# Seven-product blocks over all 16 k-tiles of gate and up, with half of the weight sums on GpSimd

## The chip, the core and the metric

The kernel runs on one core of a Trainium2 chip. Its engines work side by side, each through a queue of its own: TensorE (PE; PEld is its loading of stationary tiles), VectorE (DVE), ScalarE (ACT), GpSimd (POOL), and SyncE (SP), which here only issues transfers. The metric is the device time of one execution in microseconds; lower is better.

## The reference

A decoder trunk of two layers on 256 positions of width 2048, all in float32. Layer 0 has a Mamba-2 and an attention mixer side by side, layer 1 a stick-breaking attention; each layer ends with a gated feed-forward network (FFN) with a hidden width of 5632. Only the FFN is touched:

```python
def swiglu_ffn(h, w_gate, w_up, w_down):
    return (jax.nn.silu(h @ w_gate) * (h @ w_up)) @ w_down
...
        x = x + swiglu_ffn(rms_norm(x, ffn_norm[layer]), w_gate[layer], w_up[layer], w_down[layer])
```

## The kernel before

**Precision.** Every float32 operand is split into a high part (`hi`, `wh`) and a low part (`lo`, `wl`), and a product is hi x wh + lo x wh + hi x wl: three matmuls. For a weight tile (128 partitions x 4 k-tiles x 512 columns, 128x2048 in the profile, 1 MB) ScalarE casts `wh` out of the raw tile, and VectorE writes `wl` = raw - `wh` over the raw tile. Both are in `split`: L345 is the cast, L351 the subtraction. `wh` goes round a ring of four buffers. Raw tiles lie in slots: `w` (6), `wsum` (2), and two more (`lent`) during the FFN; a slot is used again when the last product from it is done.

**The FFN.** The 5632 hidden columns are taken in 11 blocks of 512 (`gate_up(n)`, n = 0 to 10). A block takes the 16 k-tiles of the two row tiles of x against 512 columns of gate and 512 of up. For eight k-tiles, the rows (2 x 128), the k-tiles (2 x 4) and gate/up make a 2x2 by 2x2 product, done with seven products M1 to M7 in place of eight (Winograd's form of Strassen's scheme). A product is 4 k-tiles x 3 = 12 matmuls. It needs sums of the x tiles, made once per FFN, and in every block four sums of weight tiles. With tile 11 = gate's first four k-tiles, 21 = gate's next four, 12 and 22 the same of up:

- t1 = 12 - 11 (for M5), t2 = 22 - t1 (for M6), 12 = 22 - 12 in place (for M7), t4 = 21 - t2 (for M4); M1, M2 and M3 use 11, 21 and 22.

`wsub` makes them on VectorE, L733. Blocks 0 to 2 (`HALF`) use this for k-tiles 0 to 7 and take 8 to 15 plainly (`c0` to `c3`, 24 matmuls for a tile). Blocks 3 to 10 (`MORE`) also take k-tiles 8 to 11 by seven products of two k-tiles each (`n0` to `n4`, sums `t1` to `t4` of half tiles, 128x1024), and only 12 to 15 (`c2`, `c3`) plainly. `more_sums` makes the x sums for that, on VectorE.

`left` and `right` finish a block: an add out of PSUM (L925, L930), ScalarE's Silu (L926), a product (L931) into `twins[0]` and `twins[1]`; `transpose_split` turns the result some ticks later (a tick is half a product, or one k-tile of a down). The copies of M1 and M7 wait in `twins[2]` and `twins[3]`.

**Down.** Every two blocks give eight k-tiles of the down projection: four projections of 512 columns (`project`, L456 to L459: 48 matmuls, 2 weight tiles), two of them behind each of blocks 2 to 9. ScalarE copies the result (L947) into a tile of a large pool (`s2`), and GpSimd issues a transfer that adds it to `saved` in DRAM (L948). The last three blocks' k-tiles are four projections of 12 k-tiles at the FFN's end.

**Order.** TensorE works in the order of the code. The other engines' queues are made by a scheduler from priorities: weight tiles (`wprio`) in the order of their use, `urgent` work ahead. Each queue is worked through in order.

Of the kernel before, what the change touches and what calls it, by code (L numbers as in the profile page):

```python
# [20 lines left out]
SSD_W = 2048  # L21
HID = 5632
# [25 lines left out]
class Trunk:  # L48
# [676 lines left out]
        w.left = uses  # L725
        return wh, wl, w

    def wsub(self, o, p, q, so=None, sp=None, sq=None, after=None):

        half = lambda w, n: w.raw if n is None else w.raw[:, 2 * n:2 * n + 2]  # L730
        with self.priority(self.wprio), self.tc.issue_after(after) if after else nullcontext():
            self.wprio += 100
            ins = self.nc.vector.tensor_tensor(half(o, so), half(p, sp), half(q, sq), op=ALU.subtract).ins  # L733
        for w in (p, q):
            w.readers.append(ins)
        if not o.readers:
            self.filled(o, ins)
# [11 lines left out]
    def pair(self, st, va, vb, left, right, order=HALF, after=lambda m: None, homes={}):  # L749
# [40 lines left out]
        def add(b, x, w, keep=None):  # L790

            wh, wl, slot = w
            n = len(x)
            for k, (hi, lo) in enumerate(x):
                mm(b, hi, wh[:, k])
                mm(b, lo, wh[:, k])
                if k == 1 and n > 2:
                    self.tick()
            for k, (hi, lo) in enumerate(x):
                self.clock += 1  # L800
                slot.used(mm(b, hi, wl[:, k], stop=k == n - 1), self.clock)
            self.tick()
            todo[b] -= 1
            if keep:
                with self.urgent():
                    o = kept[keep] = homes[keep] if keep in homes else self.s2([512])
                    copied = nc.scalar.copy(o, ps[b]).ins  # L807
                    if keep == "M5":
                        self.kept = copied
            with self.urgent():  # L810
                for c, q, take, t in (("p2", "M1", left, 0), ("p4", "M7", left, 1), ("z", "M5", right, 1),
                                      ("p3", "M6", right, 0)):
                    if todo[c] == 0 and q in kept:
                        todo[c] = -1
                        take(t, ps[c], kept[q])
# [27 lines left out]
        for m in order:  # L843
# [52 lines left out]
                continue  # L896
            add(bank[m], ops(m), w, m if m in keeps else None)

    def residual_back(self):
        for j in range(4):  # L900
            yield 12 if j == 0 else 6
            self.nc.gpsimd.dma_start(self.xres[j], self.saved[j])
# [12 lines left out]
    def ffn(self, layer, st, gain_next):  # L915
        nc, i = self.nc, self.i
        wg, wu, wd = i["w_gate"][layer], i["w_up"][layer], i["w_down"][layer]
        rstd = None
        h = [None, None]

        def left(t, c, s):
            nonlocal rstd
            if rstd is None:
                rstd = self.norm_end(st)
            nc.vector.tensor_tensor(s, c, s, op=ALU.add)  # L925
            nc.scalar.activation(s, s, AF.Silu, scale=rstd[:, t:t + 1])  # L926
            h[t] = s

        def right(t, c, s):
            nc.vector.tensor_tensor(s, c, s, op=ALU.add)  # L930
            nc.vector.scalar_tensor_tensor(self.twins[t].raw, s, rstd[:, t:t + 1], h[t], op0=ALU.mult, op1=ALU.mult)  # L931

        def gate_up(n):
            self.pair(st, self.cols(wg, n * 512), self.cols(wu, n * 512), left, right,
                      self.MORE if n >= 3 else self.HALF,
                      lambda m: st["lo"] if n == 0 and m in ("M3", "M6") else None,
                      {"M1": self.twins[2].raw, "M7": self.twins[3].raw})
            res = []
            return self.spawn(self.transpose_split(
                lambda t, k: self.twins[t].words[:, k * P:(k + 1) * P], res, wait=10 if n < HID // 512 - 1 else 6, rank=self.URGENT)), res  # L940

        def down(act, n0, n):
            ps = self.project(self.pairs(act), self.cols(wd, n * 512, r0=n0 * 512), 4 * len(act))
            for t in range(2):
                with self.urgent():
                    s = self.s2([512])
                    nc.scalar.copy(s, ps[t])  # L947
                nc.gpsimd.dma_start(self.saved[n][:, t], s, accum_op=ALU.add)  # L948

        act, held = [], []  # L950
        away = self.spawn(self.residual_away())
        for n in range(HID // 512):
            if n == 1:
                self.join(away)
                self.lend()
            act.append(gate_up(n))
            for c in held[:2]:
                down(*c)
            held = held[2:]
            if len(act) == 2 and n < 8:  # L960
                held = [(act, n - 1, c) for c in range(4)]
                act = []
        nst = self.norm_begin()
        self.slots["w"] = self.slots["w"][:self.LOW]
        self.slots["wsum"] = self.slots["wsum"][:self.SUMS]
# [78 lines left out]
    def norm_next(self, st, n, g):  # L1044
        if n < 2:
            self.norm_operand(st, n, g)
        else:
            self.norm_block(st, n, g, 2 if n == 2 else 6, self.URGENT)
            if n == 2:
                st["more"] = self.spawn(self.more_sums(st))  # L1050

    def out_tiles(self, g):

# [541 lines left out]
```

## Time and profile before

| | |
|---|---|
| median of 3 runs | 2374.24 us (2373.9 to 2374.75) |
| the profiled execution | 2374.79 us, of which the span of instructions 2373.1 |
| TensorE, VectorE, ScalarE, GpSimd busy | 2351.7, 1984.2, 1460.9, 207.2 us |
| mean granted TensorE clock | 0.999 |
| moved by DMA | 486.33 MB, 205 GB/s over the span |

The two FFNs take more than half of the span: layer 0's first block begins some 620 us after the start, and layer 1's ends with the kernel. A row of an engine's timeline gives start, duration, engine, line, operation, output<-inputs, shapes, how many instructions are merged into it, and in brackets the idle time before it and what ended that. Durations of neighbours overlap a little, so what an instruction costs its engine is read from start to start.

### The profile page before, as it was taken

The numbers are of one execution on the slowest core, as the hardware profiler recorded it, in microseconds if no ns is written. First come the engines' busy times: TensorE is split into PE (matmuls) and PEld (weight loads), VectorE is DVE, ScalarE is ACT, GpSimd is POOL, SyncE is SP. The second block draws the span as 40 slices with busy tenths as digits, with TensorE's granted clock in tenths as the row PEclk, the third lists the DMA queues.
The fourth block names the chain that finished last, engine by engine and source line by source line (L and its number), as shares of the span: only waits on it lengthen the run. The fifth ranks groups of instructions, "written<-read, shape, count | busy, mean of one in ns | idle before, by whom it ended". The sixth has DMA issues, their size and how long they took to land.

```text
span 2373.1 us, 28173 instructions
## 1 busy us (share of the span) xinstructions
PE 2351.7 (99%) x11083; PEld 1954.9 (82%) x11083; DVE 1984.2 (84%) x1639; ACT 1460.9 (62%) x1478; POOL 207.2 (9%) x257
## 2 busy tenths in 40 slices
PE   9999999999999999999999999999999999999998
PEld 7888888988888888888888888888888888888886
DVE  6776587588998889989888889779997988999884
ACT  6655565566665655566655786776665665556663
POOL 1342001110000000000000010000000000000011
PEclk9999999999999999999999999999999999999999
DMA  7655556545666777777676655556666777777773
GB/s 267 199 195 177 193 190 187 138 142 191 225 205 212 222 215 218 223 220 220 219 237 212 202 178 176 173 176 235 228 212 209 217 227 220 218 214 227 216 254 108
DMA packets 271396, 486.33 MB, mean 205 GB/s; under 512 B 22236, under 2 KB 47456, under 8 KB 271264
## 3 DMA queue, kind: packets, MB, share of 16 engines
q1 hardware_dynamic: 255264, 446.20, 57.3%
q0 software_dynamic: 15232, 37.01, 6.4%
q8 instruction: 87, 1.43, 0.2%
q10 hardware_dynamic: 768, 1.33, 0.2%
q14 instruction: 45, 0.37, 0.0%
HBM read 459.24 MB, written 25.20 MB: 204 GB/s over the span
## 4 chain that ended last, share of the span: by engine, by line
PE 86%; issue 7%; DVE 3%; ACT 2%; DMA 1%; POOL 0%; SPq 0%; POOLq 0%; ACTq 0%; DVEq 0%
PE acc L786 49%; PE acc L456 10%; PE acc L459 10%; PE acc L458 10%; PE tr L356 1%; ACT wh L345 1%; PE acc L500 1%; DVE w L351 1%; DVE wsum L733 1%; PE at L1445 1%; PE acc L502 0%; DVE wsum L351 0%; DMA w<-in_w_in_dram 0%; PE at L1516 0%; PE at L1517 0%
## 5 line engine op out<-in xcount | busy, mean ns | idle before, releaser
L351 DVE TENSOR_TENSOR w<-w,wh 128x2048 fp32r<-128x2048 f32 (+2 forms) x399 | 892.1, 2244 | 188.5 <-ACT wh L345 176.2
L786 PE MATMUL acc<-wh,s 128*128 128x512 f32 x3896 | 985.5, 391 | 3.7 <-ACT s L807 3.6
L345 ACT CAST wh<-w 128x2048 fp32r<-128x2048 f32 (+2 forms) x399 | 744.0, 1874 | 335.3 <-PE acc L459 139.8
L786 PEld LDWEIGHTS acc<-wh,s 128*128 128x128 f32 x3896 | 725.3, 188 | 153.9 <-ACT s L807 5.2
L456 PE MATMUL acc<-wh,s 128*128 128x512 f32 (+1 forms) x1216 | 482.9, 397 | 0.0
L459 PE MATMUL acc<-wh,s 128*128 128x512 f32 (+1 forms) x1216 | 471.3, 388 | 0.0
L458 PE MATMUL acc<-w,s 128*128 128x512 f32 (+1 forms) x1152 | 445.8, 387 | 0.5 <-DVE w L351 0.5
L786 PE MATMUL acc<-w,s 128*128 128x512 f32 x1312 | 356.0, 390 | 0.5 <-DVE w L351 0.4
L786 PEld LDWEIGHTS acc<-w,s 128*128 128x128 f32 x1312 | 246.0, 188 | 53.2 <-DVE w L351 2.0
L459 PEld LDWEIGHTS acc<-wh,s 128*128 128x128 f32 x1216 | 228.5, 188 | 47.5
L456 PEld LDWEIGHTS acc<-wh,s 128*128 128x128 f32 x1216 | 228.7, 188 | 44.9 <-issue 1.7
L458 PEld LDWEIGHTS acc<-w,s 128*128 128x128 f32 x1152 | 216.9, 188 | 42.9 <-issue 1.4
L351 DVE TENSOR_TENSOR wsum<-wsum,wh 128x2048 fp32r<-128x2048 f32 (+1 forms) x101 | 217.9, 2158 | 9.5 <-ACT wh L345 9.5
L345 ACT CAST wh<-wsum 128x2048 fp32r<-128x2048 f32 (+1 forms) x101 | 182.8, 1810 | 52.5 <-PE acc L786 23.8
L948 POOL DMA_DIRECT2D saved<-s x64 | 55.9, 995 | 1107.5 <-ACT s L947 1106.4
L345 ACT CAST wh<-lent 128x2048 fp32r<-128x2048 f32 (+1 forms) x62 | 114.6, 1858 | 61.1 <-PE acc L459 24.2
L351 DVE TENSOR_TENSOR lent<-lent,wh 128x2048 fp32r<-128x2048 f32 (+1 forms) x62 | 137.1, 2216 | 11.2 <-ACT wh L345 10.7
L733 DVE TENSOR_TENSOR wsum<-w,wsum 128x2048 f32<-128x2048 f32 (+1 forms) x52 | 104.2, 2004 | 19.9 <-PE acc L786 17.9
L786 PE MATMUL acc<-wsum,s 128*128 128x512 f32 x380 | 104.6, 390 | 1.4 <-DVE wsum L351 1.4
L786 PEld LDWEIGHTS acc<-wsum,s 128*128 128x128 f32 x380 | 71.2, 188 | 17.2 <-DVE wsum L351 2.3
L807 ACT COPY s<-acc 128x512 f32<-128x512 f32 x88 | 51.5, 587 | 39.6 <-PE acc L786 39.6
L733 DVE TENSOR_TENSOR wsum<-w,w 128x2048 f32<-128x2048 f32 (+1 forms) x35 | 71.3, 2038 | 1.4 <-DMA w<-in_w_qkv_dram 1.4
(267 smaller groups left out, 1878.6 us busy)
## 6 DMA issues: line engine op xcount, KB each, us to landing
w<-in_w_down_dram SPq DMA_DIRECT2D x80, 1024.0 KB, 5.0
w<-in_w_gate_dram SPq DMA_DIRECT2D x76, 1024.0 KB, 5.1
w<-in_w_up_dram SPq DMA_DIRECT2D x76, 1024.0 KB, 5.2
w<-in_w_qkv_dram SPq DMA_DIRECT2D x48, 1024.0 KB, 5.0
w<-in_w_in_dram SPq DMA_DIRECT2D x47, 1024.0 KB, 5.1
w<-in_w_out_even_dram SPq DMA_DIRECT2D x32, 1024.0 KB, 4.9
saved<-s POOLq DMA_DIRECT2D x64, 256.0 KB, 7.3
w<-in_w_out_odd_dram SPq DMA_DIRECT2D x16, 1024.0 KB, 5.0
```

The costliest lines, as they stand in the source:

```text
L345: cast = nc.scalar.copy(hi, src).ins
L351: return nc.vector.tensor_tensor(lo, src, hi.bitcast(F32), op=ALU.subtract).ins
L356: self.nc.tensor.transpose(out.bitcast(F32R), src, self.ident_r)
L456: nc.tensor.matmul(ps[t], hi[:, ts], wh, start=k == 0, stop=False)
L458: slot.used(nc.tensor.matmul(ps[t], hi[:, ts], wl, start=False, stop=False), self.clock)
L459: nc.tensor.matmul(ps[t], lo[:, ts], wh, start=False, stop=k == nk - 1)
L500: nc.tensor.matmul(ps[:, h % 2], wh[:, hs], x, start=k == n == 0, stop=False)
L733: ins = self.nc.vector.tensor_tensor(half(o, so), half(p, sp), half(q, sq), op=ALU.subtract).ins
L786: m = nc.tensor.matmul(ps[b], x, y, start=b not in started, stop=stop, skip_group_check=True)
L807: copied = nc.scalar.copy(o, ps[b]).ins
L948: nc.gpsimd.dma_start(self.saved[n][:, t], s, accum_op=ALU.add)
L1445: nc.tensor.matmul(py[:, ds], rows[c, h // 4][:, h % 4], xdt[c][:, ds], start=True, stop=True)
```

## The change

Blocks 3 to 10 take all 16 k-tiles by seven products: `full` does M1 to M7 for k-tiles 0 to 7 (names ending in A) and for 8 to 15 (B), 14 products. Each half has its four weight sums: t1 and t2 stay on VectorE, sum 3 (12 = 22 - 12) and t4 go to GpSimd. `second_sums` makes the x sums of the B half, its adds and subtractions on GpSimd, in place of `more_sums`. From block 3 on the slots `w` and `wsum` are one set of ten. The copies of M5 and M6 go to `twins[1]` and `twins[0]`, and `down` copies to `twins[2]` and `twins[3]` in place of `s2` tiles; the wait ahead of some transposes grows from 10 ticks to 18.

```diff
-    def wsub(self, o, p, q, so=None, sp=None, sq=None, after=None):
+    def wsub(self, o, p, q, so=None, sp=None, sq=None, after=None, engine=None):
...
-            ins = self.nc.vector.tensor_tensor(half(o, so), half(p, sp), half(q, sq), op=ALU.subtract).ins
+            ins = (engine or self.nc.vector).tensor_tensor(half(o, so), half(p, sp), half(q, sq), op=ALU.subtract).ins
...
+    FULL = ("M1A", "M5A", "M5B", "M1B", "M3A", "M3B", "M2A", "M6A", "M6B", "M2B", "M7A", "M7B", "M4A", "M4B")
+    def full(self, st, va, vb, left, right, homes):
...
+            if n == 1:
+                raw["t1" + s] = self.wtile()
+                self.wsub(raw["t1" + s], b12, b11)
+            if n == 2:
+                raw["t2" + s] = self.wtile()
+                self.wsub(raw["t2" + s], b22, raw["t1" + s])
+            if n == 3:
+                self.wsub(b12, b22, b12, engine=nc.gpsimd)
+            if n == 4:
+                raw["t4" + s] = self.wtile()
+                self.wsub(raw["t4" + s], b21, raw["t2" + s], engine=nc.gpsimd)
...
+        tile_of = {"M1": "11", "M2": "21", "M3": "22", "M4": "t4", "M5": "t1", "M6": "t2", "M7": "12"}
...
+        before = {"M1A": (lambda: load("A", "11", "12", "22"), lambda: sums("A", 1), lambda: sums("A", 2),
+                          lambda: load("B", "11", "12", "22")),
+                  "M5B": (lambda: sums("B", 1), lambda: sums("B", 2)),
+                  "M1B": (lambda: load("A", "21"), lambda: sums("A", 3)),
+                  "M3A": (lambda: load("B", "21"), lambda: sums("B", 3), lambda: sums("A", 4)),
+                  "M2A": (lambda: sums("B", 4),)}
+        for u in self.FULL:
+            for f in before.get(u, ()):
+                f()
...
+            wh, wl, slot = self.wsplit(raw[tile_of[m] + u[2]], 4, 4, mybir.DependencyClass.Sync)
+            for k, (hi, lo) in enumerate(x):
+                mm(b, hi, wh[:, k])
+                mm(b, lo, wh[:, k])
...
+            for k, (hi, lo) in enumerate(x):
+                self.clock += 1
+                slot.used(mm(b, hi, wl[:, k], stop=k == 3), self.clock)
...
+            if second and m in ("M1", "M5", "M6", "M7"):
+                with self.urgent():
+                    kept[m] = homes[m]
+                    nc.scalar.copy(kept[m], ps[b])
...
+    def second_sums(self, st):
+        pool = self.nc.gpsimd
+        sub = lambda o, p, q: pool.tensor_tensor(o, p, q, op=ALU.subtract)
+        add = lambda o, p, q: pool.tensor_tensor(o, p, q, op=ALU.add)
...
+        for k in range(2):
+            yield 1
+            a = {}
+            for j in range(2):
+                hi, lo = x[j][k]
+                r = self.s2([2, S])
+                add(r, hi.bitcast(F32), lo.bitcast(F32))
...
+            add(s1, a[1, 0], a[1, 1])
+            sub(s2, s1, a[0, 0])
+            sub(s3, a[0, 0], a[1, 0])
+            sub(s4, a[0, 1], s2)
...
+        def gate_up(n):
+            if n < 3:
+                first(n)
+            else:
+                self.full(st, self.cols(wg, n * 512), self.cols(wu, n * 512), left, right,
+                          {"M1": self.twins[2].raw, "M7": self.twins[3].raw,
+                           "M6": self.twins[0].raw, "M5": self.twins[1].raw})
...
-                    s = self.s2([512])
+                    s = self.twins[2 + t].raw
                     nc.scalar.copy(s, ps[t])
                 nc.gpsimd.dma_start(self.saved[n][:, t], s, accum_op=ALU.add)
...
+            if n == 2:
+                plain = self.slots["w"], self.slots["wsum"]
+                self.slots["w"] = self.slots["wsum"] = plain[0] + plain[1]
+                st["second"] = self.spawn(self.second_sums(st))
```

GpSimd's queue in the FFN, before: nothing but the stores of the downs, two for each.

```order
L948 DMA saved1_107<-s2_620_5905 128x512
L948 DMA saved1_107<-s2_621_5908 128x512
L948 DMA saved2_108<-s2_630_6201 128x512
L948 DMA saved2_108<-s2_631_6204 128x512
L948 DMA saved3_109<-s2_640_6281 128x512
```

After, the same queue from one block's last sum to the next block's (t4A is w9, t4B w6 in the first two rows; then sum 3 of A in lent0, the stores of the first down, sum 3 of B in wsum11, the stores of the second down, t4A in w5, t4B in w6):

```order
L733 TENSOR_TENSOR w9_80<-w5_72,wsum10_82 128x2048
L733 TENSOR_TENSOR w6_74<-lent0_110,w8_78 128x2048
L733 TENSOR_TENSOR lent0_110<-w7_76,lent0_110 128x2048
L1073 DMA saved0_106<-twin2_102 128x512
L1073 DMA saved0_106<-twin3_104 128x512
L733 TENSOR_TENSOR wsum11_84<-w4_70,wsum11_84 128x2048
L1073 DMA saved1_107<-twin2_102 128x512
L1073 DMA saved1_107<-twin3_104 128x512
L733 TENSOR_TENSOR w5_72<-w8_78,w9_80 128x2048
L733 TENSOR_TENSOR w6_74<-lent1_112,wsum10_82 128x2048
```

So each pair of stores now stands behind a sum, and the last two sums behind the second down's stores.

VectorE's queue, before, from the last weight tile of the downs into the next block: whole sums (128x2048) of k-tiles 0 to 7, half ones (128x1024) of 8 to 11, splits, and the two splits of the transposes.

```order
L351 TENSOR_TENSOR w7_75<-w7_76,wh0_65 128x2048 [waits DMAHW3_49,Activation_49]
L733 TENSOR_TENSOR wsum10_82<-w9_80,w6_74 128x2048 [waits DMAHW5_49,DMAHW4_49]
L351 TENSOR_TENSOR w6_73<-w6_74,wh1_66 128x2048 [waits Activation_49]
L733 TENSOR_TENSOR lent0_110<-w8_78,wsum10_82 128x2048 [waits DMAHW6_49,DVE_49]
L733 TENSOR_TENSOR w9_80<-w8_78,w9_80 128x2048
L351 TENSOR_TENSOR wsum10_81<-wsum10_82,wh2_67 128x2048 [waits Activation_49]
L351 TENSOR_TENSOR s2_696_7358<-tr_694_7352,s2_695_7357 128x512 [waits DMASW3_49,Activation_49]
L351 TENSOR_TENSOR s2_699_7373<-tr_697_7367,s2_698_7372 128x512 [waits Activation_49]
L733 TENSOR_TENSOR wsum11_84<-lent1_112,w5_72 128x1024 [waits DMAHW7_49,DMAHW0_49]
L733 TENSOR_TENSOR wsum11_84<-lent1_112,wsum11_84 128x1024 [waits DVE_49]
```

After, the same place (t1A is lent1, t2A w9, t1B w5, t2B wsum10; the last two rows are the splits of tiles 22A and 22B, which GpSimd's sums read):

```order
L351 TENSOR_TENSOR wsum10_81<-wsum10_82,wh0_65 128x2048 [waits DMAHW3_49,Activation_49]
L733 TENSOR_TENSOR lent1_112<-lent0_110,w8_78 128x2048 [waits DMAHW5_49,DMAHW4_49]
L733 TENSOR_TENSOR w9_80<-w7_76,lent1_112 128x2048 [waits DMAHW6_49,DVE_49]
L351 TENSOR_TENSOR w8_77<-w8_78,wh1_66 128x2048 [waits Activation_49]
L351 TENSOR_TENSOR lent1_113<-lent1_112,wh2_67 128x2048 [waits DVE_49,Activation_49]
...
L733 TENSOR_TENSOR w5_72<-wsum11_84,w6_74 128x2048 [waits DMAHW7_49,DMAHW0_49,PE_49]
L733 TENSOR_TENSOR wsum10_82<-w4_70,w5_72 128x2048 [waits DMAHW1_49,DVE_49,PE_49]
L351 TENSOR_TENSOR w5_71<-w5_72,wh3_68 128x2048 [waits DVE_49,Activation_49]
L351 TENSOR_TENSOR w6_73<-w6_74,wh0_65 128x2048 [waits Activation_49]
L351 TENSOR_TENSOR w7_75<-w7_76,wh1_66 128x2048 [waits Activation_49,Pool_49]
L351 TENSOR_TENSOR w4_69<-w4_70,wh2_67 128x2048 [waits Activation_49,Pool_49]
```

Sum 3 and the half sums have left VectorE's queue, two sums now wait for slots that PE leaves, and splits wait for GpSimd (Pool).

More of the change, by code (lines that the diff above doesn't have):

```diff
@@ L897, in pair, with load, sums, mm @@
             add(bank[m], ops(m), w, m if m in keeps else None)
+    FULL = ("M1A", "M5A", "M5B", "M1B", "M3A", "M3B", "M2A", "M6A", "M6B", "M2B", "M7A", "M7B", "M4A", "M4B")
+    def full(self, st, va, vb, left, right, homes):
+        nc = self.nc
+        raw = {}
+        def load(s, *qs):
+            for q in qs:
+                raw[q + s] = self.wload((va, vb)[int(q[1]) - 1], 8 * (s == "B") + 4 * (int(q[0]) - 1))
+        def sums(s, n):
+            b11, b12, b22, b21 = (raw.get(q + s) for q in ("11", "12", "22", "21"))
+            sync = mybir.DependencyClass.Sync
+            if n == 1:
[9 more added lines that the diff above has]
+                self.wsub(raw["t4" + s], b21, raw["t2" + s], engine=nc.gpsimd)
+        self.join(st["xT"][0][0])
+        self.join(st["xT"][1][0])
+        if "paced" in st:
+            self.join(st["paced"])
+        self.join(st["second"])
+        z, p3, p2, p4 = self.banks
+        self.banks = [p2, p3, z, p4]
+        ps = {n: self.pacc.tile([P, 512], F32, name=self.nm("acc"), tag=b, bufs=1)
+              for n, b in (("z", z), ("p3", p3), ("p2", p2), ("p4", p4))}
+        todo = {"z": 6, "p3": 4, "p2": 2, "p4": 2}
+        started, kept, halves = set(), {}, set()
+        def mm(b, x, y, stop=False):
+            m = nc.tensor.matmul(ps[b], x, y, start=b not in started, stop=stop, skip_group_check=True)
+            started.add(b)
+            return m
+        bank = {"M1": "z", "M6": "z", "M7": "z", "M5": "p3", "M3": "p3", "M2": "p2", "M4": "p4"}
+        tile_of = {"M1": "11", "M2": "21", "M3": "22", "M4": "t4", "M5": "t1", "M6": "t2", "M7": "12"}
+        place = {"M1": 0, "M2": 1, "M4": 2, "M5": 3, "M6": 4, "M7": 5, "M3": 6}
+        before = {"M1A": (lambda: load("A", "11", "12", "22"), lambda: sums("A", 1), lambda: sums("A", 2),
[7 more added lines that the diff above has]
+                f()
+            m, second = u[:2], u[2] == "B"
+            b = bank[m]
+            if second:
+                x = st["second_ops"](m)
+            else:
+                x = [tuple(o[:, k] for o in st["S"][place[m]]) for k in range(4)]
+            wh, wl, slot = self.wsplit(raw[tile_of[m] + u[2]], 4, 4, mybir.DependencyClass.Sync)
+            for k, (hi, lo) in enumerate(x):
+                mm(b, hi, wh[:, k])
+                mm(b, lo, wh[:, k])
+                if k == 1:
+                    self.tick()
+            for k, (hi, lo) in enumerate(x):
+                self.clock += 1
+                slot.used(mm(b, hi, wl[:, k], stop=k == 3), self.clock)
+            self.tick()
+            todo[b] -= 1
+            if second and m in ("M1", "M5", "M6", "M7"):
+                with self.urgent():
+                    kept[m] = homes[m]
+                    nc.scalar.copy(kept[m], ps[b])
+            with self.urgent():
+                for c, q, take, t in (("p2", "M1", left, 0), ("p4", "M7", left, 1), ("z", "M5", right, 1),
+                                      ("p3", "M6", right, 0)):
+                    if todo[c] == 0 and q in kept and (take is left or t in halves):
+                        todo[c] = -1
+                        halves.add(t)
+                        take(t, ps[c], kept[q])
@@ L931, in right, with first @@
             nc.vector.scalar_tensor_tensor(self.twins[t].raw, s, rstd[:, t:t + 1], h[t], op0=ALU.mult, op1=ALU.mult)
-        def gate_up(n):
+        def first(n):
             self.pair(st, self.cols(wg, n * 512), self.cols(wu, n * 512), left, right,
-                      self.MORE if n >= 3 else self.HALF,
+                      self.HALF,
                       lambda m: st["lo"] if n == 0 and m in ("M3", "M6") else None,
                       {"M1": self.twins[2].raw, "M7": self.twins[3].raw})
+        def gate_up(n):
+            if n < 3:
+                first(n)
+            else:
+                self.full(st, self.cols(wg, n * 512), self.cols(wu, n * 512), left, right,
+                          {"M1": self.twins[2].raw, "M7": self.twins[3].raw,
+                           "M6": self.twins[0].raw, "M5": self.twins[1].raw})
             res = []
             return self.spawn(self.transpose_split(
-                lambda t, k: self.twins[t].words[:, k * P:(k + 1) * P], res, wait=10 if n < HID // 512 - 1 else 6, rank=self.URGENT)), res
+                lambda t, k: self.twins[t].words[:, k * P:(k + 1) * P], res, wait=6 if n == HID // 512 - 1 else 18 if n in (3, 5, 7) else 10, rank=self.URGENT)), res
         def down(act, n0, n):
@@ L963, in ffn @@
         nst = self.norm_begin()
-        self.slots["w"] = self.slots["w"][:self.LOW]
-        self.slots["wsum"] = self.slots["wsum"][:self.SUMS]
+        self.slots["w"] = plain[0][:self.LOW]
+        self.slots["wsum"] = plain[1][:self.SUMS]
         self.spawn(self.residual_back())
```

19 lines of the change are left out of this document (17 added, 2 removed).

## The prediction

> **What bounds the kernel now.** I read the page's engine shares and chain first, then the time between the down projections' stores, then one block's stretch by engine, then single rows of that block.
>
> ```profile
> PE 2351.7 (99%) x11083; PEld 1954.9 (82%) x11083; DVE 1984.2 (84%) x1639; ACT 1460.9 (62%) x1478; POOL 207.2 (9%) x257
> PE 86%; issue 7%; DVE 3%; ACT 2%; DMA 1%; POOL 0%; SPq 0%; POOLq 0%; ACTq 0%; DVEq 0%
> ...
> 749.19 1.80 POOL L948 DMA_DIRECT2D saved<-s  x2 [131.88 <-ACT s L947]
> ...
> 1183.08 1.75 POOL L948 DMA_DIRECT2D saved<-s  x2 [46.18 <-ACT s L947]
> ...
> core 0: us, PE busy (x) PEld busy (x) DVE busy (x) ACT busy (x) POOL busy (x), PEclk, DMA share, GB/s
> 873.10:935.10 62.00, 62.00 (x280) 51.33 (x279) 55.26 (x34) 37.55 (x30) 3.49 (x4) 1.00 0.71 221
> 2067.00:2129.00 62.00, 62.00 (x280) 51.33 (x279) 54.32 (x32) 37.55 (x29) 3.49 (x4) 1.00 0.73 221
> ```
>
> TensorE is busy 99% and is 86% of the chain. Seven blocks (n = 3 to 9, each with two down projections behind it) lie between the two stores: (1183.08 - 749.19) / 7 = 61.98 us a block. In such a stretch the columns are length, PE, PEld, DVE, ACT, POOL: PE fills all 62.0, VectorE 55.3, ScalarE 37.6, GpSimd 3.5, at a granted clock of 1.00. PE bounds the block; VectorE has 6.7 us to spare. That small reserve is what this change is about.
>
> ```profile
> 878.28 1.28 DVE L351 TENSOR_TENSOR s<-tr,s 128x512 fp32r<-128x512 f32 x2
> 879.48 1.21 DVE L733 TENSOR_TENSOR wsum<-w,w 128x1024 f32<-128x1024 f32 x1
> 880.72 1.23 DVE L733 TENSOR_TENSOR wsum<-w,wsum 128x1024 f32<-128x1024 f32 x1
> 881.87 1.22 DVE L733 TENSOR_TENSOR w<-w 128x1024 f32<-128x1024 f32 x1
> ...
> 893.60 2.28 DVE L351 TENSOR_TENSOR wsum<-wsum,wh 128x2048 fp32r<-128x2048 f32 x1
> 895.80 2.28 DVE L351 TENSOR_TENSOR w<-w,wh 128x2048 fp32r<-128x2048 f32 x1
> ...
> 922.09 0.68 DVE L930 TENSOR_TENSOR s<-acc,s 128x512 f32<-128x512 f32 x1
> 922.69 2.28 DVE L351 TENSOR_TENSOR w<-w,wh 128x2048 fp32r<-128x2048 f32 x1
> ...
> 925.49 1.40 DVE L931 SCALAR_TENSOR_TENSOR twin<-s,rstd,twin 128x512 f32<-128x512 f32 x2
> ...
> 890.60 1.92 ACT L345 CAST wh<-w 128x2048 fp32r<-128x2048 f32 x1
> ...
> 884.42 1.98 PE L786 MATMUL acc<-wh,s 128*128 128x512 f32 x8
> 886.23 1.07 PE L786 MATMUL acc<-w,s 128*128 128x512 f32 x4
> 887.14 1.98 PE L786 MATMUL acc<-wh,s 128*128 128x512 f32 x8
> ```
>
> From start to start a full split or sum costs VectorE 2.20 (893.60 to 895.80), a half one 1.15 (880.72 to 881.87), an add out of PSUM 0.60 (922.09 to 922.69), the two splits of a block's transposes 1.20 (878.28 to 879.48). One product of 4 k-tiles is 12 matmuls, 884.42 to 887.14: 2.72 us, 0.2267 each.
>
> **The change, part by part.** TensorE: a block of today has 7 products on k-tiles 0 to 7, 7 half ones, and 2 weight tiles taken plainly: 84 + 42 + 48 = 174 matmuls, and two downs add 96. 270 x 0.2267 = 61.2, and the transposes make up the 0.8 to 62.0. The new block has 14 x 12 = 168, so 60.65 with its downs: 1.36 less. Over 16 such blocks (8 in each FFN) that is 21.8 us, if PE stays the bound.
>
> VectorE: full splits go from 12 to 14 and the one half split goes; sums on it go from 4 full and 4 half to 4 full. That is +2 x 2.20 - 5 x 1.15 = -1.35, so 55.3 becomes 53.9 of its own work. ScalarE: 1.5 more casts of 1.9 us, 37.6 + 2.9 = 40.5 of 60; its idle time covers them. Loads: the same 12 tiles a block, covered as before, since a block doesn't get much shorter in any case.
>
> GpSimd: four sums of 128x2048 a block. No row of before has this size. The nearest are its smaller tensor_tensors, undisturbed:
>
> ```profile
> 252.61 2.56 POOL L1201 TENSOR_TENSOR twin<-s,twin 128x512 f32<-128x512 f32 x2 [27.39 <-ACT twin L408]
> 461.23 0.45 POOL L1348 TENSOR_TENSOR ropeb<-s,rope 128x128 f32<-128x128 f32 x1
> ```
>
> 1.28 for 512 columns and 0.45 for 128 give 0.00216 a column, so 1.28 + 1536 x 0.00216 = 4.6 us for 2048, twice what VectorE takes. 4 x 4.6 = 18.4 a block would be harmless on an idle engine, if it ran beside VectorE. These rows say that it doesn't:
>
> ```profile
> 297.72 2.55 POOL L1201 TENSOR_TENSOR twin<-s,twin 128x512 f32<-128x512 f32 x2 [19.91 <-ACT twin L408]
> 299.05 1.77 DVE L351 TENSOR_TENSOR s<-s,s 128x512 fp32r<-128x512 f32 x1 [2.68 <-POOL twin L1201]
> ...
> 2315.32 2.55 POOL L992 TENSOR_TENSOR s<-xres,s 128x512 f32<-128x512 f32 x2 [31.86 <-DVE xres L989]
> 2317.17 2.85 DVE L351 TENSOR_TENSOR w<-w,wh 128x2048 fp32r<-128x2048 f32 x1 [1.25 <-ACT wh L345]
> ...
> 492.65 0.51 POOL L1347 TENSOR_TENSOR ropea<-s,rope 128x128 f32<-128x128 f32 x1
> 492.76 2.54 DVE L733 TENSOR_TENSOR wsum<-w,wsum 128x2048 f32<-128x2048 f32 x1
> ...
> 169.78 2.42 DVE L351 TENSOR_TENSOR w<-w,wh 128x2048 fp32r<-128x2048 f32 x1 [0.57 <-ACT wh L345]
> 170.02 3.34 POOL L1452 TENSOR_TENSOR s<-s,s 128x512 f32<-128x512 f32 x1
> ...
> 101.94 4.53 POOL L1421 TENSOR_TENSOR s<-s,s 128x512 f32<-128x512 f32 x2 [2.12 <-ACT s L1420]
> 103.98 2.02 DVE L1369 SCALAR_TENSOR_TENSOR s<-tr,vb,s 128x255 f32<-128x255 f32 x5
> ```
>
> ```profile
> L351 DVE TENSOR_TENSOR s<-s,s 128x512 fp32r<-128x512 f32 x43 | 30.3, 712 | 6.3 <-ACT s L345 3.7 <-POOL twin L1201 2.7
> ```
>
> First pair: a split of 128x512, 0.71 on the mean, starts at 299.05 just as the second GpSimd instruction does and takes 1.77: held for 1.06, until 0.14 before GpSimd's end. Second: 2.85 for 2.29, held for 0.56, again until 0.14 before the end. Third: behind a short GpSimd instruction the hold is short, 0.25, to 0.15 before its end. Fourth: the split was first, and GpSimd takes 3.34 = its 1.28 and the 2.06 that were left of the split. So a VectorE instruction with both inputs in SBUF and a GpSimd tensor_tensor take turns, each whole. Last pair: VectorE instructions that read one input from PSUM (tr) are not held, 0.40 each as ever.
>
> How long a 4.6 us instruction holds VectorE, no row shows. The ends: 1.06, the longest hold seen, and 4.6, all of it. At two lengths (0.5 and 1.28) the hold ran to the GpSimd instruction's end, so I take 4.6. On that the sign hangs: 4 x 1.06 makes VectorE's block 58.1, under PE's 60.65; 4 x 4.6 makes it 72.3. The Trainium skill ("SBUF — State Buffer", Who interferes with whom) says that the second of two such instructions "fully blocks" for all of the first, which bears out the larger end for a length that this trace doesn't hold; by it the block is the 72.3, by the longest hold seen it is PE's 60.65.
>
> The steady block then: of VectorE's 53.9, 4 adds of 0.60 and the transposes' two splits, 1.2, read PSUM and can lie beside GpSimd: 3.6. So the block takes 50.3 + 18.4 = 68.7 if all of them do, 72.3 if none; I take the middle, 70.5: 8.5 more than 62.0. It is bound by VectorE and GpSimd in turn, and PE waits for the low parts (L351). Seven such blocks: +59.5.
>
> Block n = 10 has no downs behind it whose 21.8 us of PE time could be drawn on: 14 splits and 4 sums (39.6), the adds and the two products of L931 (3.7), 43.3, and 18.4, less the same half: 59.9, against 174 x 0.2267 + 0.8 = 40.2. +19.7 (17.8 to 21.5). The last four projections (72 matmuls to 3 splits) are PE's again, unchanged.
>
> Once per FFN: second_sums puts 4 adds of 512 columns (1.28) and 8 of 256 (0.73 by the same line) on GpSimd, 11 us, in place of more_sums on VectorE; and splits made ahead when block 3 begins feed PE for up to three products, 8 us. Together -8 to +11, taken as 0.
>
> The added waits. The splits of tiles 22, 21 and t2 now wait for GpSimd's sums, since they overwrite what those read, and all later splits stand behind them on VectorE. While VectorE waits so, GpSimd runs the sum undisturbed: the 4.6 us are paid once, as a hold or as this wait, and not counted twice. Sum t2B goes to a slot that the last weight tile of the downs leaves when PE is done with it, so VectorE can be at most two splits ahead when a block begins; with a backlog of 8.5 us it comes there after PE and doesn't wait. On GpSimd's queue each pair of stores of a down now stands behind a sum, and ScalarE's copies into the twins wait for the store before to land:
>
> ```profile
> DMA to landing us min/median/max: 5.5/7.3/8.7
> ```
>
> A copy follows 10.9 us (48 x 0.2267) after the copy that filled the same twin. Two issues of 0.9 and 7.3 leave 1.8 us of room; a sum of 4.6 that begins late uses it up, and the casts behind the copy on ScalarE wait for the rest, 2.8 us and more. I count nothing for it in the middle case: GpSimd's sum for the other block half runs in that time anyway.
>
> Sum: 2 x (59.5 + 19.7 + 0) = +158 against the profiled execution's 2374.8 (span 2373.1; the median of the runs is 2374.2, which is the same within 0.03%): **2533**. Ends: 2 x (7 x 6.7 + 17.8 - 8) = +113, 2488; and 2 x (7 x 10.3 + 21.5 + 11) = +209, 2584.
>
> **The rivals.** (1) Short holds: a long GpSimd instruction gives VectorE way before its end. Up to a hold of (60.65 - 53.9) / 4 = 1.7 us a sum, PE stays the bound and the time is 2374.8 - 21.8 = 2353, faster. For it: the longest hold seen is 1.06. Against it: every hold ran to within 0.15 of the end. (2) Holds of half the length, 9.2 a block: 53.9 + 9.2 - 1.8 = 61.3, a gain of 0.7 in seven blocks, and in block 10 50.7 for 40.2: 2 x (10.5 - 4.9) = +11, 2386. (3) Late stores: the sums come so late that the copies into the twins hold ScalarE at both downs of every block, 2 x 2.8 = 5.6 us more in 14 blocks: 2533 + 78 = 2611. For it: the order puts a sum ahead of each pair. Against it: VectorE has a backlog of its own then.
>
> **How the numbers follow.** The middle case gets 0.70, (3) 0.13, (2) 0.07, (1) 0.10. About 0.2% is what a measurement of this kernel can tell from no change. Half of (2)'s small chance lies near it: faster 0.11, same 0.03, slower 0.86. The range takes in the middle case and (3): up to 2615. Down, it goes past 2488 to three quarters of the hold, 13.8 a block: 2 x (7 x 3.9 + 15.1) = +84, 2459. That leaves out (1) and (2), 0.17.
>
> **What would show it.** Right: GpSimd sums of 4.6 us, some 7 where they come second; VectorE splits of 4 to 7 us beside them; PE busy some 60 of about 70 us a block, its idle time ended by DVE L351; VectorE busy nearly all of the block, holds included. Wrong: splits at 2.29 beside running sums (1); blocks of 62 (2); ScalarE waiting for the stores (3), or for loads into the ten slots. A sum on GpSimd far from 4.6 moves all of it: 1 us each is 16 blocks x 4 = 64 us.

## The result and the profile after

The changed kernel takes 2559.86 us (median of 5 runs, 2558.73 to 2563.57) against 2374.23 (5 runs): the ratio is 1.0785, 95% interval 1.0769 to 1.0801. The profiled execution took 2559.65, of which the span is 2557.9, 184.8 more than the span before.

The page's first part (engine, busy us, share of the span, instructions), and the stores of the first down behind block 2 and of the first down behind block 9, seven blocks later, as GpSimd's timeline has them:

```profile
PE 2401.7 (94%) x10987; PEld 1972.7 (77%) x10987; DVE 2246.1 (88%) x1591; ACT 1500.5 (59%) x1504; POOL 627.4 (25%) x345
...
754.71 1.82 POOL L1073 DMA_DIRECT2D saved<-twin  x2 [3.03 <-ACT twin L1072]
...
1270.27 1.75 POOL L1073 DMA_DIRECT2D saved<-twin  x2
```

TensorE is no longer full: 94%. VectorE is busy for 262 us more than before though it has 48 instructions fewer, and GpSimd for 420 more. The page's own chain is of no use here; it is cut off after a few per cent of the span. So the blocks are read in windows. (Between the two stores it is 73.65 us a block.) From the first matmul of block 3 to the first of block 10 are seven blocks; the windows view gives length, PE, PEld, VectorE, ScalarE, GpSimd:

```profile
core 0: us, PE busy (x) PEld busy (x) DVE busy (x) ACT busy (x) POOL busy (x), PEclk, DMA share, GB/s
762.05:1276.38 514.33, 456.55 (x1906) 367.85 (x1904) 497.81 (x210) 280.17 (x210) 189.26 (x56) 0.94 0.60 186
```

514.33 / 7 = 73.48 us a block, where it was 61.98. VectorE is busy 497.81 / 7 = 71.12 of it. Its 210 instructions, 30 a block, would fill 54 us at their usual lengths (a run below measures that); the rest is time in which they are held. One block shows it; VectorE's rows and GpSimd's (start, duration, engine, line, operation, output<-inputs):

```profile
907.62 2.28 DVE L733 TENSOR_TENSOR wsum<-lent,w 128x2048 f32<-128x2048 f32 x1
909.99 6.78 DVE L733 TENSOR_TENSOR w<-w,wsum 128x2048 f32<-128x2048 f32 x1
...
919.08 2.28 DVE L351 TENSOR_TENSOR w<-w,wh 128x2048 fp32r<-128x2048 f32 x1
921.28 6.72 DVE L351 TENSOR_TENSOR lent<-lent,wh 128x2048 fp32r<-128x2048 f32 x1
...
909.99 4.63 POOL L733 TENSOR_TENSOR lent<-w,lent 128x2048 f32<-128x2048 f32 x1 [6.13 <-DVE wsum L733]
...
921.24 4.62 POOL L733 TENSOR_TENSOR wsum<-w,w 128x2048 f32<-128x2048 f32 x1 [4.93 <-PE acc L937]
925.82 6.62 POOL L733 TENSOR_TENSOR w<-w,w 128x2048 f32<-128x2048 f32 x1
```

The sum at 909.99 starts with GpSimd's, takes 6.78 for 2.28, and so is held for 4.50 of GpSimd's 4.63. The split at 921.28 is held for 4.44. The GpSimd sum at 925.82 came second: it stands through the rest of VectorE's instruction and takes 6.62. For these instructions it is two engines, one at a time.

TensorE in the same stretch, and its largest waits over the whole run (engine, output, line, what ended the wait: us, times, longest):

```profile
913.42 1.98 PE L937 MATMUL acc<-wh,s 128*128 128x512 f32 x8
919.22 1.93 PE L937 MATMUL acc<-wsum,s 128*128 128x512 f32 x4 [3.82 <-DVE wsum L351]
920.95 2.88 PE L937 MATMUL acc<-wh,s 128*128 128x512 f32 x8
...
928.05 1.20 PE L937 MATMUL acc<-lent,s 128*128 128x512 f32 x4 [1.47 <-DVE lent L351]
...
934.65 2.08 PE L937 MATMUL acc<-w,s 128*128 128x512 f32 x4 [3.58 <-DVE w L351]
936.52 3.56 PE L937 MATMUL acc<-wh,s 128*128 128x512 f32 x8
...
PE acc L937 <- DVE w L351: 88.6, 34, 4.6
PE acc L937 <- DVE wsum L351: 26.9, 8, 4.6
PE acc L937 <- DVE lent L351: 14.2, 6, 3.6
```

Three times in the block TensorE runs out of low parts and waits for a split (L351). None of its waits in these blocks ended on a load.

### The profile page after: what moved, and what is told of

The parts are those of the page before. It is cut to its first block, busy times and chain, and to the rows that moved or that the text cites. A ratio compares the mean times of both kernels' runs of the same rounds, so it can differ in the third digit from the quotient of the medians.

```text
span 2557.9 us, 28167 instructions
## 1 busy us (share of the span) xinstructions
PE 2401.7 (94%) x10987; PEld 1972.7 (77%) x10987; DVE 2246.1 (88%) x1591; ACT 1500.5 (59%) x1504; POOL 627.4 (25%) x345
## 5 line engine op out<-in xcount | busy, mean ns | idle before, releaser
L351 DVE TENSOR_TENSOR w<-w,wh 128x2048 fp32r<-128x2048 f32 (+2 forms) x419 | 1084.0, 2603 | 163.4 <-ACT wh L345 152.8
L345 ACT CAST wh<-w 128x2048 fp32r<-128x2048 f32 (+2 forms) x419 | 779.2, 1874 | 292.2 <-DVE w L733 90.5
L458 PE MATMUL acc<-w,s 128*128 128x512 f32 (+1 forms) x1056 | 408.2, 387 | 0.1
L351 DVE TENSOR_TENSOR wsum<-wsum,wh 128x2048 fp32r<-128x2048 f32 x103 | 272.1, 2644 | 9.4 <-ACT wh L345 9.0
L345 ACT CAST wh<-wsum 128x2048 fp32r<-128x2048 f32 x103 | 196.8, 1911 | 126.5 <-DVE wsum L733 42.2
L937 PE MATMUL acc<-w,s 128*128 128x512 f32 x560 | 168.3, 426 | 88.6 <-DVE w L351 88.6
L786 PE MATMUL acc<-w,s 128*128 128x512 f32 x784 | 210.6, 390 | 0.5 <-DVE w L351 0.4
L351 DVE TENSOR_TENSOR lent<-lent,wh 128x2048 fp32r<-128x2048 f32 x56 | 151.5, 2711 | 2.8 <-ACT wh L345 2.8
L345 ACT CAST wh<-lent 128x2048 fp32r<-128x2048 f32 x56 | 107.1, 1912 | 74.0 <-DVE w L351 37.4
L733 POOL TENSOR_TENSOR w<-wsum,w 128x2048 f32<-128x2048 f32 x12 | 75.7, 6323 | 161.9 <-DVE lent L733 144.5
L733 DVE TENSOR_TENSOR w<-w,w 128x2048 f32<-128x2048 f32 x29 | 103.3, 3564 | 0.5
```

The lines of the kernel that those rows point to most:

```text
L345: cast = nc.scalar.copy(hi, src).ins
L351: return nc.vector.tensor_tensor(lo, src, hi.bitcast(F32), op=ALU.subtract).ins
L458: slot.used(nc.tensor.matmul(ps[t], hi[:, ts], wl, start=False, stop=False), self.clock)
L733: ins = (engine or self.nc.vector).tensor_tensor(half(o, so), half(p, sp), half(q, sq), op=ALU.subtract).ins
L786: m = nc.tensor.matmul(ps[b], x, y, start=b not in started, stop=stop, skip_group_check=True)
L937: m = nc.tensor.matmul(ps[b], x, y, start=b not in started, stop=stop, skip_group_check=True)
```

## The experiments

Four explanations stood at the start. The letters are those of the expectations. H, the holds: while GpSimd reads SBUF, VectorE's two-input work stands still, so GpSimd's sums cost VectorE more than making them itself. S: the 14 products on one set of ten slots cost the time, whoever makes the sums. D: the added waits and the order on GpSimd's queue do. C: TensorE's slower clock behind each wait does, in large part. All sums are of 128x2048. A time without an interval is of one run; the kernel before took 2374.15 to 2374.18 beside these runs.

**All sums back on VectorE.**

```diff
-                self.wsub(b12, b22, b12, engine=nc.gpsimd)
+                self.wsub(b12, b22, b12)
...
-                self.wsub(raw["t4" + s], b21, raw["t2" + s], engine=nc.gpsimd)
+                self.wsub(raw["t4" + s], b21, raw["t2" + s])
```

> Sum 3 and t4 go back to VectorE; the 14 products, the ten slots and second_sums stay as changed. Theory H (a GpSimd sum holds VectorE for its whole length): VectorE's own work is 53.9 + 4 x 2.2 = 62.7 us a block, against PE's 60.65, so blocks of 61 to 65 us in place of 73.5, and 2374.8 + 16 x (-0.7 to 3) + 5 = 2370 to 2430 us. Rival S (14 products in a row out of ten slots starve PE by themselves): gate and up stays near the 51 us of the changed kernel, and the time within 30 of 2560.

Measured: 2417.18 us, ratio 1.0179 (1.0164 to 1.0194). S falls: with the same 14 products and ten slots 143 of the 186 us are gone. What is left over the kernel before is mostly VectorE's own work, 435.41 / 7 = 62.2 of 64.0 us a block. A small part of S is real here: of the 12.8 us that VectorE is idle over the seven blocks, 8.1 are waits for gate tiles to land, 1.2 us a block. The seven blocks:

```profile
763.73:1211.95 448.22, 432.25 (x1905) 353.41 (x1904) 435.41 (x237) 282.43 (x211) 24.43 (x28) 0.99 0.68 214
```

**GpSimd writes, but reads nothing.** Each of its sums becomes two fills of the same tile, so that the dependencies, the queue order and most of the length (2 x 1.8 us for 4.6) stay.

```diff
+            if engine is None:
+                ins = self.nc.vector.tensor_tensor(half(o, so), half(p, sp), half(q, sq), op=ALU.subtract).ins
+            else:
+                first = engine.memset(half(o, so), 0.0).ins
...
+                ins = engine.memset(half(o, so), 0.0).ins
```

> Leaves out: each GpSimd sum is replaced by two fills with zero of the same tile, so that GpSimd writes as much but reads nothing; places in the queue and waits stay. Theory H, with the hold coming from the second reading port: VectorE's splits stay at 2.28 us beside the fills, PE is the bound, and the time is 2374.8 - 21.8 + 5 = 2350 to 2365. Rival D (it is the waits for GpSimd and the stores that stand behind the sums): with fills of 3 to 5 us a pair, 2450 to 2560. Rival A (any GpSimd instruction holds VectorE): splits grow by the length of a fill, 2450 to 2560.

Measured: 2359.05 us, 15 less than before the change. A VectorE sum and the fill beside it, and the seven blocks:

```profile
870.34 2.29 DVE L734 TENSOR_TENSOR w<-lent,w 128x2048 f32<-128x2048 f32 x1
870.42 1.81 POOL L736 MEMSET wsum<- 128x2048 f32 x1 [32.17 <-DVE w L734]
...
761.91:1186.23 424.32, 424.32 (x1905) 351.29 (x1904) 378.15 (x211) 281.43 (x211) 124.99 (x85) 1.00 0.71 226
```

TensorE is busy for the whole of 424.32 / 7 = 60.62 us a block, 1.36 less than 61.98, the gain that the prediction had worked out for a kernel bound by TensorE. D falls, and so does A of this expectation, that any GpSimd instruction holds VectorE: GpSimd is busy for 125 us here and the sum beside its fill takes its usual 2.29; VectorE's own work is 378.15 / 7 = 54.0.

**GpSimd reads one input.** A copy of its first input in place of each sum.

```diff
+            if engine is None:
+                ins = self.nc.vector.tensor_tensor(half(o, so), half(p, sp), half(q, sq), op=ALU.subtract).ins
+            else:
+                ins = engine.tensor_copy(half(o, so), half(p, sp)).ins
```

> Each of GpSimd's sums is a copy of its first input, 128x2048 (one input in SBUF in place of two; the sums' values are left out). Theory 'two inputs lock': a one-input operation doesn't hold VectorE, the time is that of the fills, 2359 (2350 to 2375). Theory 'any long read locks': gate and up take 38.1 + 3 x the copy's length; at 2 us or more a copy that is 2359 + 16 x 6 = 2455 or more, at 4.6 us 2560.

Measured: 2389.11 us. The rows of one copy and of the VectorE sum beside it, and the seven blocks:

```profile
887.07 1.90 POOL L736 COPY lent<-w 128x2048 f32<-128x2048 f32 x1 [6.12 <-DVE wsum L734]
...
887.10 4.01 DVE L734 TENSOR_TENSOR w<-w,wsum 128x2048 f32<-128x2048 f32 x1
...
763.27:1200.67 437.40, 430.02 (x1905) 349.76 (x1904) 418.44 (x211) 277.23 (x210) 104.73 (x56) 1.00 0.70 219
```

A copy reads one input only, and still holds VectorE: 4.01 for 2.28, so 1.73 of its 1.90 us. "Two inputs lock" is wrong; a GpSimd instruction that reads only one input from SBUF holds VectorE too. The price that the other theory gave, 2455 or more, was too high as well: four such holds bring VectorE to 59.8 us a block, only just what TensorE needs (60.62), and the block becomes 62.5. The Trainium skill ("SBUF — State Buffer", Who interferes with whom) states the rule that way round: a VectorE instruction with two SBUF inputs contends with a GpSimd instruction that reads SBUF, and not with one that only writes it. The fills, the copies and the sums here agree with it: held for 0, for 1.73 of 1.90 and for 4.50 of 4.63 us.

**More of the same cost.** Sum 3 is made twice in place (which changes its value), six GpSimd sums a block instead of four.

```diff
                 self.wsub(b12, b22, b12, engine=nc.gpsimd)
+                self.wsub(b12, b22, b12, engine=nc.gpsimd)
```

> Leaves out the value: sum 3 is made twice in place (which gives the old tile 12 back), so that GpSimd has 6 sums a block. Theory H: 2 more holds of 4.5 us in 16 blocks, +144 if none of it is hidden, +60 if the ones that fall into the down projections are: 2620 to 2705. Rival D (only waits for a sum's result count): nothing waits for tile 12 before M7, so 2560 to 2580.

Measured: 2699.02 us, 139 more than the changed kernel.

```profile
763.23:1336.03 572.80, 467.25 (x1906) 373.21 (x1905) 557.23 (x211) 279.97 (x211) 268.74 (x70) 0.89 0.55 168
```

VectorE is busy 557.23 / 7 = 79.6 of 81.8 us a block with one instruction more in all seven: two sums added 8.5 of busy time and 8.35 of block, 4.2 each. That is inside H's range, and D's 2560 to 2580 is far off. The cost follows the number of GpSimd's sums.

**TensorE kept warm.** Idle matmuls (8, 4 and 5) behind the high products at which it then waits, into a bank that nothing reads.

```diff
+            fill = self.tr([512]) if u in ("M5B", "M3A", "M3B") else None
+            for _ in range({"M5B": 8, "M3A": 4, "M3B": 5}.get(u, 0)):
+                nc.tensor.matmul(fill, self.ident_r, wh[:, 0], start=True, stop=True)
```

> The changed kernel, with idle matmuls (8, 4 and 5 of 512 columns, into a tile that nobody reads) on PE behind the high products of M5B, M3A and M3B, where it stalls. Theory C (behind a stall of 3.6 us PE runs some 12 matmuls at half speed, of which about 2.5 us a block lie on the path): without the dip 2560 - 16 x (1.5 to 3.5) = 2504 to 2536. Rival V (VectorE's holds set the pace of a block whatever PE's clock does): 2555 to 2565, or more where the idle matmuls delay a product.

Measured: 2555.98 us, ratio 1.0764 (1.0746 to 1.0782). Its seven blocks, and a stretch of one block:

```profile
763.27:1274.33 511.06, 472.02 (x2025) 379.86 (x2024) 496.56 (x210) 279.91 (x210) 190.31 (x56) 0.97 0.60 187
...
833.70:907.50 73.80, 66.60 (x298) 53.64 (x298) 71.73 (x33) 41.05 (x32) 27.19 (x8) 1.00 0.61 187
```

The granted clock goes from 0.94 to 0.97 over the seven, in the one block to 1.00, and a block takes 511.06 / 7 = 73.0 for 73.5, in the one with the full clock no less. C falls, with a time 20 us above its highest figure, and V holds: TensorE's slow matmuls lie mostly in time that it would spend waiting for VectorE anyway.

**One GpSimd sum at a time.** Two theories of where a hold costs: P, only in gate and up, since TensorE doesn't need VectorE in the downs; T, wherever it falls, since VectorE's total is the bound. First sum 3 of A alone on GpSimd, whose hold falls in the downs:

```diff
-                self.wsub(b12, b22, b12, engine=nc.gpsimd)
+                self.wsub(b12, b22, b12, engine=nc.gpsimd if s == "A" else None)
...
-                self.wsub(raw["t4" + s], b21, raw["t2" + s], engine=nc.gpsimd)
+                self.wsub(raw["t4" + s], b21, raw["t2" + s])
```

> Only sum 3 of A stays on GpSimd; sum 3 of B and both t4 sums go back to VectorE. In the changed kernel this sum holds VectorE (6.71 us for a split of 2.2) at the end of a block, while TensorE does the down projections. Theory P (a hold costs where it falls; VectorE has room in the downs): no more than all sums on VectorE, 2417, and down to 2417 - 16 x 2.2 = 2382 where the sum taken off VectorE counts too: 2380 to 2420. Theory T (VectorE's total, holds included, is the bound wherever they fall): 62.7 + 4.5 - 2.2 = 65.0 us of VectorE a block, 2417 + 16 x 2.3 = 2454 (2440 to 2465).

Then t4 of B alone, whose hold falls in gate and up:

```diff
-                self.wsub(b12, b22, b12, engine=nc.gpsimd)
+                self.wsub(b12, b22, b12)
...
-                self.wsub(raw["t4" + s], b21, raw["t2" + s], engine=nc.gpsimd)
+                self.wsub(raw["t4" + s], b21, raw["t2" + s], engine=nc.gpsimd if s == "B" else None)
```

> Only the sum t4 of B stays on GpSimd; its hold falls in the gate and up part of a block. Both theories: the hold of 4.5 us in place of VectorE's own 2.2, 2417 + 16 x 2.3 = 2454 (2440 to 2465). Only if a single GpSimd sum goes beside VectorE for nothing: 2417 - 16 x 2.2 = 2382. Read against the run with sum 3 of A alone: theory P says that this one is slower by 30 us or more, theory T says that the two are the same.

Measured: 2427.04 us, ratio 1.0220 (1.0203 to 1.0237), and 2447.63 in one run. Neither theory has both. Their seven blocks, sum 3 of A first:

```profile
764.42:1218.38 453.96, 433.89 (x1906) 351.22 (x1905) 451.64 (x231) 279.98 (x210) 70.25 (x35) 0.99 0.68 211
```

```profile
764.33:1225.76 461.43, 437.05 (x1905) 356.70 (x1904) 446.96 (x231) 278.41 (x210) 71.67 (x35) 0.98 0.66 207
```

With sum 3 of A on GpSimd VectorE's busy time goes from 62.2 to 64.5 us a block: 2.3, just T's hold of 4.5 less the 2.2 that VectorE no longer spends itself. P falls: the hold in the downs is not free, because VectorE works through the downs on the next block's sums and splits. But T's time, 2454, was too high. With all sums on VectorE it was idle for 1.8 us a block (64.0 less 62.2), in this run for 0.3 (64.85 less 64.5); the rest of the hold went into that idle time. In the other run the idle time stays at 2.1 (65.9 less 63.85), and the block is longer. VectorE's waits over the seven blocks say part of why. With all sums on VectorE 8.1 of its 12.8 idle us are the waits for gate tiles; with sum 3 of A on GpSimd no such wait is left, so the hold seems to have taken their place. With t4 of B on GpSimd VectorE's busy time goes up by only 1.65 a block, but it waits once for GpSimd's sum, for 4.5 us, and 3.2 us for gate tiles, of 14.5 idle us in all. So a sum on GpSimd costs VectorE more than its own 2.2 in both places, as a hold or as a wait, and the block as much as VectorE's idle time doesn't take up. Each place was tried with one sum only.

**Short pieces.** Each GpSimd sum in four pieces of 128x512.

```diff
+                for k in range(4):
+                    ins = engine.tensor_tensor(o.raw[:, k], p.raw[:, k], q.raw[:, k], op=ALU.subtract).ins
...
```

> Each of GpSimd's sums in four pieces of 128x512. Theory 'turns, whole': the pieces hold VectorE for the same total (4 x 1.28 = 5.1 a sum in place of 4.6), but one after another over several VectorE instructions: 2555 to 2610. Rival 'one long hold starves TensorE, short ones are absorbed by the splits made ahead': clearly less, 2400 to 2520.

Measured: 2555.24 us, 0.2% under the changed kernel's 2559.86. The pieces of one sum (min/median/max in ns), VectorE's rows beside that sum, its largest waits in the seven blocks, and these blocks:

```profile
L737 POOL TENSOR_TENSOR lent<-w,lent x4: 3333/3338/3347, 909.6 to 919.5; 128x512 f32<-128x512 f32 x4
...
914.97 3.39 DVE L351 TENSOR_TENSOR w<-w,wh 128x2048 fp32r<-128x2048 f32 x1
918.28 3.38 DVE L351 TENSOR_TENSOR lent<-lent,wh 128x2048 fp32r<-128x2048 f32 x1
922.83 2.29 DVE L351 TENSOR_TENSOR w<-w,wh 128x2048 fp32r<-128x2048 f32 x1 [1.18 <-POOL lent L737]
...
DVE w L351 <- POOL w L737: 28.0, 10, 4.9
DVE wsum L351 <- POOL w L737: 14.6, 4, 4.9
DVE w L351 <- POOL wsum L737: 10.9, 3, 4.9
...
764.01:1272.76 508.75, 454.16 (x1906) 356.06 (x1904) 436.99 (x209) 277.18 (x210) 296.67 (x140) 0.96 0.61 187
```

The engines now alternate, one piece and one split: a piece of 1.28 takes 3.34, a split of 2.28 takes 3.39. VectorE's busy time falls to 436.99 / 7 = 62.4, but the sum is done later, and the split that overwrites what the sum reads waits for it, (28.0 + 14.6 + 10.9) / 7 = 7.6 us a block. Together they come to 70.0, with 1.8 of waits for ScalarE and 0.5 for another sum to 72.3, and the block is 72.7. The exclusive time was shared out otherwise and not saved; "one long hold starves TensorE" falls.

No version that computes the whole result came under the kernel before. Four sums a block cost VectorE 8.8 us if it makes them, and some 17 if GpSimd does; of all the runs only the one in which they cost VectorE nothing, 2359, was faster. How much they may cost before the gain is gone no run shows, but four holds by copies, of up to 1.73 us each, are already too much.

## Why the prediction was right, and where its sum was off

It said 2533 (2459 to 2615) and slower; it is 2559.86. The mechanism was the one forecast, and nearly all excess lies in blocks 3 to 10. Two terms were off, in opposite directions.

- **TensorE's gain, 1.36 us a block, and VectorE's own work, 53.9.** Right: the run with fills, in which nothing holds VectorE, has blocks of 60.62 (61.98 less 1.36), with 54.0 of VectorE's work.
- **A GpSimd sum of 4.6 us.** Right. GpSimd's sums of two forms in the trace (ns, min/median/max; first and last start; form):

```profile
L733 POOL TENSOR_TENSOR lent<-w,lent x12: 4612/4624/6580, 732.2 to 2433.7; 128x2048 f32<-128x2048 f32 x12
L733 POOL TENSOR_TENSOR wsum<-lent,wsum x4: 6566/6570/6572, 895.6 to 2345.3; 128x2048 f32<-128x2048 f32 x4
```

  4.62 undisturbed, up to 6.6 where it comes second.
- **The hold, taken as the whole length.** Right: 4.50 of 4.63, until 0.13 before GpSimd's end, as with the short instructions of the kernel before. The larger of the two ends decided the sign, as the prediction said it would.
- **The steady block, 70.5.** This is the term that was mis-sized; it measured 73.5. VectorE's part is 71.1: 54.0 and four holds that cost 4.3 each on the mean, 17.1 of the 18.4. The prediction had 16.6 for them, since it let half of the 3.6 us of work that reads PSUM lie beside GpSimd. The rows show little of that: one split of a transpose, 0.6, in every second block, where the hold is then 3.8. The other holds are some 4.4, because each ends 0.1 to 0.2 before its sum does. But the larger part is that the block was set equal to VectorE's busy time. It has 2.4 us of waits besides, 16.5 over the seven blocks, 15.0 of them behind ScalarE and most of these at the end of gate and up. VectorE's waits in these blocks, and the place in one of them:

```profile
DVE w L351 <- ACT wh L345: 8.6, 9, 1.1
DVE twin L1048 <- ACT twin L1043: 5.6, 7, 0.8
DVE wsum L351 <- ACT wh L345: 0.8, 2, 0.5
...
951.15 0.68 DVE L1042 TENSOR_TENSOR twin<-acc,twin 128x512 f32<-128x512 f32 x1
952.63 0.75 DVE L1048 SCALAR_TENSOR_TENSOR twin<-twin,rstd,twin 128x512 f32<-128x512 f32 x1 [0.79 <-ACT twin L1043]
954.43 2.29 DVE L351 TENSOR_TENSOR w<-w,wh 128x2048 fp32r<-128x2048 f32 x1 [1.05 <-ACT wh L345]
```

  VectorE's add goes to ScalarE's activation (L1043) and back, 0.79, and the next split's cast stands behind that activation, 1.05. While TensorE sets the block such waits cost nothing: in the run with fills VectorE waits for ScalarE for 24 us over its seven blocks, and TensorE is full. Once VectorE sets the block they add to it. That they do is read from the sum (71.1 and 2.4 are the 73.5); no run takes these waits away. The prediction's upper end for the block, 72.3, left it out and was passed.
- **Block 10, +19.7.** Mis-sized the other way: its gate and up took 39.44 us from first matmul to the downs before, and 49.97 now (1276.38 to 1326.35), +10.5, under the lower bound of 17.8. The prediction said that no downs stand behind this block to draw on. But what a block draws on are the downs ahead of it, and block 10 has them: VectorE makes its first sums there, at 1261.25 and 1263.56, and is idle for 0.03 of the 22.53 us of these downs. So its gate and up takes nearly what that of blocks 3 to 7 takes, 50.7 to 51.9. By the prediction's own numbers the term would have been 70.5 - 21.8 - 40.2 = 8.5. Gate and up of block 6, and the downs between it and block 7, in which VectorE (third busy time) is never idle:

```profile
981.67:1032.62 50.95, 42.81 (x178) 34.09 (x176) 48.91 (x22) 31.87 (x24) 18.84 (x5) 0.93 0.60 196
1032.62:1055.14 22.52, 22.52 (x106) 18.65 (x104) 22.49 (x12) 9.28 (x9) 8.29 (x3) 1.00 0.62 164
```

- **The start of an FFN, 0.** Blocks 0 to 2 end 1.6 us later, within the bounds given. The sum is then 2 x (7 x 11.5 + 10.5 + 1.6) = +185, the 184.8 that the span grew by. That the total came within 27 us of the forecast is in part luck: the two errors, +21 and -9 in each FFN, have opposite signs. Without the second it would have been some 2578. That too is under the upper end, 2584, though the steady block alone passed its bound, because that end also put 11 us on the start of each FFN, of which 1.6 came.
- **Rivals.** (1) and (2), short or half holds, fall with the 4.50; the time of (1), 2353, is nearly what the kernel does when GpSimd reads nothing, 2359. A hold of 1.7 a sum was said to be the point up to which TensorE stays the bound. The copies hold VectorE for up to 1.73, and the block was 62.5 against 60.6. In that run VectorE also waits 12.8 us for ScalarE over the seven blocks, 1.8 a block, so the point lies lower, at (60.65 - 53.9 - 1.8) / 4 = 1.2 a sum as an estimate. (3), late stores, did not happen. The only wait of ScalarE in the whole run that ended on a store is this one:

```profile
ACT twin L972 <- DMA saved<-twin: 0.7, 1, 0.7
```

  Against it the prediction had put that VectorE would have a backlog, so that nothing behind the sums is in a hurry; that agrees with the trace, where VectorE is busy 71.1 of 73.5 us a block.

## What to carry to other kernels

Count the time in which GpSimd reads SBUF as VectorE's time, wherever VectorE's own work has two SBUF inputs: a sum moved from VectorE to GpSimd then costs VectorE about 4.3 us in place of 2.2, and is no relief. An engine with 6.7 us of reserve in a 62 us block becomes the bound quickly, and then waits come onto the path that were hidden before (here 2.4 us a block, nearly all of them VectorE's waits for ScalarE): set the new block to its busy time and these waits together, which fits this case and was not tried on another. Where work runs ahead, look at which stage lies ahead of a block, and not behind it, to see from which time it can draw.

## What the runs showed of the hardware

- A GpSimd fill of 128x2048 (1.81 us) holds nothing, a copy (1.90 us) holds VectorE's two-input work for 1.73, and a sum (4.63 us) for 4.50. Among these three, what counts is that GpSimd reads SBUF, not how many inputs it has.
- Between back-to-back instructions of both engines the turn changes after each one: pieces of 1.28 took 3.34, and the VectorE instructions between them 3.39.
- Behind waits of TensorE of 3.56 to 4.63 us the next 6 to 12 matmuls run at about half rate (8 in 3.56 at 936.52, 1.98 elsewhere), at a granted clock of 0.93 to 0.95 over a block; behind waits of 1.09 to 1.47 they don't. In between the length alone doesn't decide. Two places of the changed kernel, slow behind 2.28 and at full rate behind 2.40:

```profile
771.75 1.34 PE L937 MATMUL acc<-w,s 128*128 128x512 f32 x4 [2.28 <-DVE w L351]
772.88 3.47 PE L937 MATMUL acc<-wh,s 128*128 128x512 f32 x8
...
845.06 1.20 PE L937 MATMUL acc<-w,s 128*128 128x512 f32 x4 [2.40 <-DVE w L351]
846.10 1.99 PE L937 MATMUL acc<-wh,s 128*128 128x512 f32 x8
```

  In the run with idle matmuls 8 took 3.07 behind a wait of only 2.18. So no threshold is read from this. The Trainium skill ("TensorE: Matmul & The Clock Gate", HAM oscillation — how this bites in real kernels) asks for no gaps over about 3.4 us. The slow matmuls behind 3.56 us and more agree with that; those behind 2.28 and 2.18 do not follow from it. The slow clock cost next to nothing here, as the run with idle matmuls shows, since TensorE was not the bound.
